# Row sums added on GpSimd and fetched a pair ahead, top-level scores as full products, in a hybrid GLA and NSA layer

## The chip, the core and the metric

The kernel runs on one core of a Trainium2 chip. The metric is device time in microseconds of one execution of the whole layer. Three runs of the kernel before took 1116.94 to 1117.36 us, with a median of 1117.23 us.

The core has TensorE for matrix products, and three engines for elementwise work: VectorE, ScalarE and GpSimd. The profile calls them PE (and PEld for TensorE's weight loads), DVE, ACT and POOL. SyncE (SP) only issues DMA transfers here. Each engine works off its own queue in order, and waits on semaphores for the others.

## The reference

One layer over 256 tokens of width 2048: a gated linear attention (GLA) with 4 heads and a native sparse attention (NSA) with 8 heads read one normalised input through one projection, their outputs go through one output projection, and a SwiGLU feed-forward network (FFN) with 5632 hidden columns follows. Cut to what matters here:

```python
def hybrid_layer(x, ...):
    n = rms_norm(x, attn_norm_g)
    proj = n @ w_in
    ...
    h = x + jnp.concatenate([gla_out, nsa_out], axis=-1) @ w_out
    m = rms_norm(h, ffn_norm_g)
    return h + (jax.nn.silu(m @ w_gate) * (m @ w_up)) @ w_down
```

and of the GLA mixer the scores, which decay with the distance of key and query:

```python
    decay = jnp.exp(jnp.where(causal, b[:, :, :, None, :] - b[:, :, None, :, :], -jnp.inf))
    scores = jnp.einsum('bhtd,bhsd,bhtsd->bhts', qi, ki, decay)
```

## The kernel before

All arrays are fp32. A product of fp32 values is made of three products of a rounded part (hi) and a rest (lo): hi x hi, hi x lo and lo x hi. So each piece of a weight matrix is loaded, rounded by ScalarE (`act(..., AF.Copy)`, lines L136 and L623) and subtracted by VectorE (L137 and L624), before TensorE can use it.

**The stages.** The input projection runs in column blocks of 512 (`proj`), each over four chunks of four row tiles (`chunk`, whose matmuls are L282). The mixers (`gla_mix`, `nsa_mix`) are generators: `drive` (L97) takes a step of them between the matmuls of a chunk, so that their small operations lie under the projections. Then come the output projection (`w_out_half`) and the FFN, which loops over 11 blocks of 512 hidden columns: `gate_up` (products at L1073), `turn_act`, and `down` of the block before (L282 again). In the program's text the operations have this order; the order in each engine's queue is settled when the kernel is built, by a scheduler that may move independent operations past each other. `behind(op)` tells it to place an operation after another.

**Seven products in place of eight.** For a pair of row tiles of the FFN's first product, `gate_up` treats the 2 x 2 tiles of tokens and the 2 x 2 tiles of weights (two of w_gate, two of w_up) as small matrices, and multiplies them with seven products in place of eight (`sevens`). That needs four sums of weight tiles. Where there are none ready, VectorE makes them at the pair (L1104 to L1106): one of 1024 elements a partition and two of 512. `parts_of2` then takes both halves of the sums into hi and lo.

**Row sums made early.** For the blocks 5 to 10 and the pairs 2, 5 and 7 (`SUMS`) these sums are made long before, behind the mixers: 18 generators `sum_rows` (L1003) wait in `background`, and `drive` takes a step of one of them whenever it has counted `rate` units. Each loads two tiles of w_gate and two of w_up from SP's queue (L1009, two transfers of 512 KB), adds in four steps of 512 elements a partition (L1014, on VectorE, each placed behind VectorE's newest subtraction), and stores the two results to DRAM from GpSimd's queue (L1018, two transfers of 512 KB). In the FFN, `gate_up` fetches them back at the pair itself from SP's queue (L1099), right behind the pair's weights (L1041), whose last quarter is then not needed.

**Buffers.** Tiles of 4 KB a partition come from the 24 buffers `g4`. In the FFN, 22 of them are held by the tokens, their forms, the residual and the activations, so that two are left for the first half of a pair's sums; the second half has the two buffers `fsum`. The weights have three buffers `fraw`, their hi and lo parts four buffers `ftwo`.

**GpSimd's other work.** Its queue carries a few masks and memsets, and the power of -1/2 that makes a reciprocal root (`rsqrt_`, L212): 14 short operations on 1 to 8 elements a partition, most of them in the normalisations of the mixers. VectorE waits for each of them.

**Scores by levels.** `gla_scores` (L556) makes the scores of a tile of 128 queries and 128 keys from eight products, one for each level of a binary split (1, 2, 4, to 64), and picks from each the part that belongs to it. Of the top level only the quarter of the 64 first keys and the 64 last queries is used (L574), and only that quarter is computed (L565); the others are full products of 128 x 128 (L567). There are 8 such tiles.

Of the kernel before, what the change touches and what calls it, by code (L numbers as in the profile page):

```python
# [12 lines left out]
ALU = mybir.AluOpType  # L13
AX = mybir.AxisListType

P = 128
# [20 lines left out]
def kernel(  # L37
# [4 lines left out]
    nc = tc.nc  # L42
    act, mm = nc.scalar.activation, nc.tensor.matmul
    TT, TS, STT = nc.vector.tensor_tensor, nc.vector.tensor_scalar, nc.vector.scalar_tensor_tensor
# [13 lines left out]
    def slot(pool, tag, bufs, align=None):  # L58
        def f(shape, dt=F32):
            n_tiles[0] += 1  # L60
            return pool.tile([P] + list(shape), dt, tag=tag, bufs=bufs, name=f"{tag}_{n_tiles[0]}", align_bytes=align)
        return f
# [3 lines left out]
    g4, g2, g1, small = slot(gp, "g4", 24, LINE), slot(s2p, "g2", 13), slot(s1p, "g1", 7), slot(s1p, "sm", 12)  # L66

    def bank():
        n_tiles[0] += 1
        return pp.tile([P, 512], F32, tag="bank", name=f"bank_{n_tiles[0]}")  # L70

    def behind(op):

        return tc.issue_after(op.ins) if op is not None else nullcontext()
# [17 lines left out]
    def drain(queue):  # L92
        while queue:
            for _ in queue.pop(0):
                pass
# [17 lines left out]
    last = {}  # L113
# [442 lines left out]
    def gla_scores(h, b, res):  # L556
        tb = slice(b * P, (b + 1) * P)
        sc, e = g1([P]), dec[h // 2]
        for half in range(2):
            p = bank()  # L560
            for j in range(4):
                l = LEVELS[4 * half + j]
                u, w = (e[l][:, h % 2, tb],) * 2 if l else (kT[:, h, tb], qT[:, h, tb])
                if 2 * l == P:
                    mm(p[:l, j * P + l:(j + 1) * P], u[:, :l], w[:, l:], start=True, stop=True)  # L565
                else:
                    mm(p[:, j * P:(j + 1) * P], u, w, start=True, stop=True)  # L567
                yield
            for j in range(4):
                l, pl = LEVELS[4 * half + j], p[:, j * P:(j + 1) * P]  # L570
                if l == 0:
                    TT(sc, pl, lmask[:, 0, :], ALU.mult)
                elif 2 * l == P:
                    nc.vector.tensor_copy(sc[:l, l:], pl[:l, l:])  # L574
                else:
                    nc.vector.copy_predicated(sc, lmask[:, 4 * half + j, :].bitcast(mybir.dt.uint32), pl)
        res["s"] = sc
# [423 lines left out]
    row_sums = {}  # L1001

    def sum_rows(f, pair):  # L1003

        n_tiles[0] += 1
        gate, up = g4([2, 512]), g4([2, 512])
        for to, m in ((gate, w_gate), (up, w_up)):
            with behind(last["dma"]):
                nc.sync.dma_start(to, m[0][2 * pair * P:(2 * pair + 2) * P, f * FB:(f + 1) * FB].rearrange("(k p) w -> p k w", p=P))  # L1009
        for _ in range(3):  # L1010
            yield True
        for o, i in ((up[:, 0], up[:, 1]), (up[:, 1], gate[:, 1]), (gate[:, 1], up[:, 0]), (gate[:, 0], gate[:, 1])):
            with behind(last["d"]):
                TT(o, o, i, ALU.add)  # L1014
            yield True
        to = row_sums[f, pair] = [dp.tile([P, 2, 512], F32, name=f"sums{i}_{f}_{pair}") for i in range(2)]
        for part, a in zip(to, (up, gate)):
            nc.gpsimd.dma_start(part, a)  # L1018
        for _ in range(1):
            yield True  # L1020
# [3 lines left out]
    fw = {}  # L1024
# [12 lines left out]
    def load4(parts):  # L1037

        r, at = fw["raw"]([4, 512]) if fw else weight("raw", 4, 512, 3, F32), 0
        for mat, k0, nk, c0 in parts:  # L1040
            nc.sync.dma_start(r[:, at:at + nk], mat[k0 * P:(k0 + nk) * P, c0:c0 + 512].rearrange("(k p) w -> p k w", p=P))  # L1041
            at += nk
        return r
# [14 lines left out]
    def parts_of2(s1, s2):  # L1058
# [2 lines left out]
            in_parts(hi[:, 2 * i:2 * i + 2], lo[:, 2 * i:2 * i + 2], v)  # L1061
        return [(hi[:, k], lo[:, k]) for k in range(4)]


    banks = {}

    def gate_up(fb):
        def product(q, a, w, k):

            if q not in banks:  # L1070
                banks[q] = bank()
            for x, m in ((a[0], w[k][0]), (a[0], w[k][1]), (a[1], w[k][0])):
                mm(banks[q], x, m, start=todo[q] == total[q], stop=todo[q] == 1)  # L1073
                todo[q] -= 1

        def tokens(k, t):
            assert k in turned
            return tuple(x[k // 4][:, k % 4, t * P:(t + 1) * P] for x in (hT_h, hT_l))

        order, sevens = (ORDER0, ORDER1, ORDER)[0 if fb == 0 else 1 if fb < ALL7 else 2], FIRST7.get(fb, PAIRS7)  # L1080
        last7 = max(sevens, key=order.index)
        todo = dict.fromkeys((1, 5, 6, 7), 3 * len(sevens))
        todo.update(dict.fromkeys((2, 3, 4), 3 * len(sevens) + 6 * (8 - len(sevens))))
        todo[8] = 6 * (8 - len(sevens))
        total = dict(todo)
        if fb > 1:
            urgent.append(turn_act(fb - 1, (8, 8)))
        for at, pair in enumerate(order):
            if fb > 1 and pair not in sevens:
                drain(urgent)  # L1090
            if fb == 0 and at == len(OLD):
                ffn_pools()
            a, b = 2 * pair, 2 * pair + 1
            ready = row_sums.get((fb, pair))
            r = load4([(w_gate[0], a, 2, fb * FB), (w_up[0], a, 1 if ready else 2, fb * FB)])
            if ready:
                sums = s1, s2 = g4([2, 512]), (fw["sum"] if fw else g4)([2, 512])
                for to, part in zip(sums, ready):
                    nc.sync.dma_start(to, part)  # L1099
            if pair in sevens:  # L1100
                w = parts_of(r[:, 0:3])
                if not ready:
                    s1, s2 = g4([2, 512]), fw["sum"]([2, 512])
                    TT(s1, r[:, 1:3], r[:, 3:4].to_broadcast([P, 2, 512]), ALU.add)  # L1104
                    TT(s2[:, 0], s1[:, 1], r[:, 1], ALU.add)  # L1105
                    TT(s2[:, 1], s2[:, 0], r[:, 0], ALU.add)  # L1106
                f = [tuple(forms[pair][:, i, j] for i in range(2)) for j in range(4)]
                raw = {1: (tokens(b, 0), 1), 2: (tokens(a, 0), 0), 3: (f[3], 2)}
                of_sums = {5: (f[0], 0), 7: (f[2], 1), 6: (f[1], 2), 4: (tokens(a, 1), 3)}

                for q in (6, 1, 5, 7, 2, 3, 4) if at == 7 else (1, 2, 3, 5, 7, 6, 4):
                    if q in of_sums and len(of_sums) == 4:
                        ws = parts_of2(s1, s2)
                        if ready:
                            ws = [ws[k] for k in (1, 0, 3, 2)]
                    if q in raw:
                        x, k = raw[q]
                        product(q, x, w, k)
                    else:
                        x, k = of_sums.pop(q)  # L1120
                        product(q, x, ws, k)
                    yield 2
            else:
                w = parts_of(r)
                for q, t, m in ((2, 0, 0), (3, 0, 1), (4, 1, 0), (8, 1, 1)):
                    for j in range(2):
                        product(q, tokens(a + j, t), w, 2 * m + j)
                        yield 2
            if pair == last7:
                q1, u, q5u, q7u, q57u = (g2([512]) for _ in range(5))  # L1130
                act(q1, banks[1], AF.Copy)
                TT(u, banks[6], q1, ALU.add)
                TT(q5u, banks[5], u, ALU.subtract)
                TT(q7u, banks[7], u, ALU.add)  # L1134
                TT(q57u, banks[5], q7u, ALU.subtract)
                if fb == 1:
                    urgent.append(turn_act(0, (1, 5)))
                if fb:
                    seed(0, DOWN[min(fb - 1, 1)])
        if fb == 0:  # L1140
            drain(urgent)
            rms(rf, ssh)
            TT(rf, rf, hback, ALU.mult)
        gs = hidden[fb] = []
        for t, (g, gq, u_, uq) in enumerate(((q1, 2, q5u, 3), (q7u, 4, q57u, 8))):
            TT(g, banks[gq], g, ALU.add)
            act(g, g, AF.Silu, scale=rf[:, t:t + 1])
            if total[uq]:
                TT(u_, banks[uq], u_, ALU.add)
            STT(g, u_, rf[:, t:t + 1], g, ALU.mult, ALU.mult)  # L1150
            gs.append(g)
# [184 lines left out]
```

## Time and profile before

| | us |
|---|---|
| median of 3 runs | 1117.23 |
| the profiled execution | 1116.86 |
| its span, first to last instruction | 1115.2 |
| TensorE busy (PE) | 1106.1 |
| VectorE busy (DVE) | 993.3 |
| ScalarE busy (ACT) | 741.0 |
| GpSimd busy (POOL) | 50.1 |

The profile is that of one execution. A line of its groups reads: line of the kernel, engine, operation, what it writes and reads by the program's names, shapes, count; then the busy time of the group, the mean duration of one in ns, and the idle time of the engine just before them with what ended it. A line of a timeline gives start, duration, engine, line, operation, and in brackets the idle time before it with its releaser. A line of the chain of waits gives start, duration, and who did the work which the end waited for; followed back from the last instruction, these pieces fill the whole span. "issue" is time in which an engine waited for nothing that the profile shows. A matmul's duration overlaps the next one's, since they are pipelined; two starts lie closer together than the mean duration says. The granted clock of TensorE was 1.00 throughout.

### The profile page before, as it was taken

The page shows a single profiled execution, that of the slowest core. Times are in us where ns is not written, and L with a number is a line of the kernel's source. Part 1 is how long each engine was busy: PE and PEld are TensorE (multiplying, and loading weights), DVE is VectorE, ACT ScalarE, POOL GpSimd, SP SyncE. Part 2 cuts the span into 40 slices and gives each one's busy share as a digit, 9 for nine tenths or more (in the row PEclk, how much of TensorE's full clock was granted, in tenths as well). Part 3 has the DMA queues.
Part 4 walks back from the last instruction along what each step waited for, and adds up shares of the span by engine and source line. Part 5 has one row for each costly group of instructions (what it writes and reads, how often), then busy time and mean ns, then how long its engine had stood idle before and what let it go on. Part 6 is the DMA issues. An engine that isn't in the chain of part 4 may idle for free.

```text
span 1115.2 us, 14712 instructions
## 1 busy us (share of the span) xinstructions
PE 1106.1 (99%) x5354; PEld 908.0 (81%) x5354; DVE 993.3 (89%) x1294; ACT 741.0 (66%) x1001; POOL 50.1 (4%) x97
## 2 busy tenths in 40 slices
PE   9999999999999999999999999999999999999998
PEld 8888887898778887887888888888888788888886
DVE  6678779987588889999899999899999999999997
ACT  7655557544576486657586676768686776768694
POOL 3110000111001000000000000000000000000000
PEclk9999999999999999999999999999999999999999
DMA  7999984475884786646465746767666767766763
GB/s 272 346 343 368 354 284 167 136 247 179 274 303 165 240 303 223 239 175 236 154 214 178 244 159 212 249 227 249 233 245 237 262 207 274 256 245 229 250 226 113
DMA packets 127795, 265.39 MB, mean 238 GB/s; under 512 B 6838, under 2 KB 8922, under 8 KB 127723
## 3 DMA queue, kind: packets, MB, share of 16 engines
q1 hardware_dynamic: 121642, 244.50, 63.4%
q0 software_dynamic: 5184, 18.88, 4.2%
q10 hardware_dynamic: 896, 1.07, 0.3%
q8 instruction: 42, 0.69, 0.2%
q14 instruction: 31, 0.25, 0.1%
HBM read 243.45 MB, written 20.97 MB: 237 GB/s over the span
## 4 chain that ended last, share of the span: by engine, by line
PE 94%; DVE 2%; ACT 2%; DMA 1%; issue 1%; POOL 0%; ACTq 0%; POOLq 0%; DVEq 0%
PE bank L282 46%; PE bank L1073 39%; PE bank L209 3%; PE bank L1214 2%; PE bank L883 1%; PE bank L567 1%; DVE lo L137 1%; PE bank L821 1%; DMA raw<-in_w_in_dram 1%; DMA raw<-in_w_out_dram 0%; ACT hi L136 0%; PE bank L737 0%; ACT ftwo L623 0%; POOL sm L212 0%; PE bank L824 0%
## 5 line engine op out<-in xcount | busy, mean ns | idle before, releaser
L1073 PE MATMUL bank<-ftwo,g 128*128 128x512 f32 x1848 | 431.7, 393 | 0.2 <-ACT ftwo L623 0.2
L1073 PEld LDWEIGHTS bank<-ftwo,g 128*128 128x128 f32 x1848 | 342.0, 188 | 77.1 <-DVE ftwo L624 3.1
L282 PE MATMUL bank<-hi,g 128*128 128x512 f32 (+2 forms) x1088 | 323.5, 376 | 0.0
L624 DVE TENSOR_TENSOR ftwo<-fraw,ftwo 128x1536 fp32r<-128x1536 f32 (+1 forms) x130 | 256.9, 1983 | 7.1 <-ACT ftwo L623 6.1
L623 ACT ACTIVATE ftwo<-fraw 128x1536 fp32r<-128x1536 f32 (+1 forms) x130 | 216.4, 1669 | 26.5 <-DMA fraw<-in_w_up_dram 10.0
L282 PE MATMUL bank<-ftwo,g 128*128 128x512 f32 x960 | 221.2, 390 | 0.4 <-ACT g L623 0.4
L282 PEld LDWEIGHTS bank<-hi,g 128*128 128x128 f32 x1088 | 192.4, 188 | 30.7 <-issue 1.0
L282 PEld LDWEIGHTS bank<-ftwo,g 128*128 128x128 f32 x960 | 179.5, 188 | 39.4 <-ACT bank L1185 1.3
L136 ACT ACTIVATE hi<-raw 128x1024 fp32r<-128x1024 f32 (+3 forms) x124 | 130.1, 1056 | 106.4 <-PE bank L282 62.7
L282 PE MATMUL bank<-lo,g 128*128 128x512 f32 (+3 forms) x544 | 195.3, 377 | 1.2 <-DVE lo L137 1.0
L137 DVE TENSOR_TENSOR lo<-raw,hi 128x1024 fp32r<-128x1024 f32 (+3 forms) x124 | 150.1, 1218 | 37.1 <-ACT hi L136 32.3
L623 ACT ACTIVATE ftwo<-g 128x1024 fp32r<-128x1024 f32 x74 | 78.3, 1058 | 75.9 <-DVE g L1104 60.4
L282 PEld LDWEIGHTS bank<-lo,g 128*128 128x128 f32 x544 | 98.5, 188 | 16.9 <-DVE lo L137 2.0
L624 DVE TENSOR_TENSOR ftwo<-g,ftwo 128x1024 fp32r<-128x1024 f32 x74 | 90.3, 1220 | 15.7 <-ACT ftwo L623 15.7
L624 DVE TENSOR_TENSOR ftwo<-fsum,ftwo 128x1024 fp32r<-128x1024 f32 x74 | 90.3, 1220 | 0.3
L623 ACT ACTIVATE ftwo<-fsum 128x1024 fp32r<-128x1024 f32 x74 | 77.6, 1050 | 4.5 <-DVE fsum L1106 3.3
L1197 ACT COPY g<-bank 128x512 f32<-128x512 f32 x80 | 46.0, 587 | 43.8 <-PE bank L282 41.9
L1104 DVE TENSOR_TENSOR g<-fraw 128x1024 f32<-128x1024 f32 x54 | 65.3, 1219 | 0.3 <-issue 0.3
L1185 ACT COPY bank<-g 128x512 f32<-128x512 f32 x80 | 45.0, 590 | 10.7 <-DVE f L1134 9.1
L623 ACT ACTIVATE g<-bank 128x512 fp32r<-128x512 f32 (+1 forms) x50 | 29.0, 591 | 32.8 <-PE bank L209 22.3
L1106 DVE TENSOR_TENSOR fsum<-fsum,fraw 128x512 f32<-128x512 f32 x54 | 37.2, 688 | 0.8
L1105 DVE TENSOR_TENSOR fsum<-g,fraw 128x512 f32<-128x512 f32 x54 | 37.1, 688 | 0.8
(235 smaller groups left out, 873.8 us busy)
## 6 DMA issues: line engine op xcount, KB each, us to landing
fraw<-in_w_gate_dram SPq DMA_DIRECT2D x86, 512.0 KB, 3.7
fraw<-in_w_down_dram SPq DMA_DIRECT2D x42, 1024.0 KB, 5.1
raw<-in_w_in_dram SPq DMA_DIRECT2D x36, 1024.0 KB, 6.9
fraw<-in_w_up_dram SPq DMA_DIRECT2D x68, 512.0 KB, 4.7
sums<-g POOLq DMA_DIRECT2D x36, 512.0 KB, 6.6
raw<-in_w_out_dram SPq DMA_DIRECT2D x16, 1024.0 KB, 6.2
g<-in_w_gate_dram SPq DMA_DIRECT2D x18, 512.0 KB, 7.6
g<-in_w_up_dram SPq DMA_DIRECT2D x18, 512.0 KB, 8.2
```

What stands on the lines that cost most here:

```text
L136: act(h[:, i:i + n], r[:, k + i:k + i + n], AF.Copy)
L137: last["d"] = TT(o[:, i:i + n], r[:, k + i:k + i + n], f32(h[:, i:i + n]), ALU.subtract)
L209: return nc.tensor.transpose(o, i, ident[:n, :n])
L282: last["mm"] = mm(bk[t], a[:, k, t * P:(t + 1) * P], m[:, off:off + w], start=(first_ and k == 0 and i == 0), stop=(end and k == 3 and i = ...
L623: act(hi, ps, AF.Copy)
L624: last["d"] = TT(lo, ps, f32(hi), ALU.subtract)
L1073: mm(banks[q], x, m, start=todo[q] == total[q], stop=todo[q] == 1)
L1104: TT(s1, r[:, 1:3], r[:, 3:4].to_broadcast([P, 2, 512]), ALU.add)
L1105: TT(s2[:, 0], s1[:, 1], r[:, 1], ALU.add)
L1106: TT(s2[:, 1], s2[:, 0], r[:, 0], ALU.add)
L1185: nc.scalar.copy(banks[qs[n][t]], h_sb[n][:, t, :])
L1197: nc.scalar.copy(h_sb[n][:, t, :], bs[t])
```

## The change

Three edits:

- The four additions of `sum_rows` run on GpSimd in place of VectorE, and are no longer placed behind an operation of VectorE.
- The sums are fetched by `fetch_sums`, from GpSimd's queue in place of SP's, and a pair ahead: at the start of a pair, for the pair after it. The buffers for them are taken then.
- The top level's score product is computed in full (128 x 128) like the others; the part that is used stays the same.

```diff
@@ gla_scores
-                if 2 * l == P:
-                    mm(p[:l, j * P + l:(j + 1) * P], u[:, :l], w[:, l:], start=True, stop=True)
-                else:
-                    mm(p[:, j * P:(j + 1) * P], u, w, start=True, stop=True)
+                mm(p[:, j * P:(j + 1) * P], u, w, start=True, stop=True)
@@ sum_rows
         for o, i in ((up[:, 0], up[:, 1]), (up[:, 1], gate[:, 1]), (gate[:, 1], up[:, 0]), (gate[:, 0], gate[:, 1])):
-            with behind(last["d"]):
-                TT(o, o, i, ALU.add)
+            nc.gpsimd.tensor_tensor(o, o, i, ALU.add)
             yield True
@@ new
+    fetched = {}
+
+    def fetch_sums(fb, pair):
+
+        if (fb, pair) in row_sums:
+            to = fetched[fb, pair] = g4([2, 512]), fw["sum"]([2, 512])
+            for a, part in zip(to, row_sums[fb, pair]):
+                nc.gpsimd.dma_start(a, part)
@@ gate_up
             ready = row_sums.get((fb, pair))
+            if at < 7:
+                fetch_sums(fb, order[at + 1])
             r = load4([(w_gate[0], a, 2, fb * FB), (w_up[0], a, 1 if ready else 2, fb * FB)])
             if ready:
-                sums = s1, s2 = g4([2, 512]), (fw["sum"] if fw else g4)([2, 512])
-                for to, part in zip(sums, ready):
-                    nc.sync.dma_start(to, part)
+                s1, s2 = fetched.pop((fb, pair))
```

The new lines shift the numbers of the lines behind them: L1014 becomes L1010, L1018 becomes L1014, L624 becomes L621.

## The prediction

> **What bounds the kernel now.** I read the page's first part and its chain of waits, then the busy time by stretch, then the chain in order of time.
>
> ```profile
> span 1115.2 us, 14712 instructions
> PE 1106.1 (99%) x5354; PEld 908.0 (81%) x5354; DVE 993.3 (89%) x1294; ACT 741.0 (66%) x1001; POOL 50.1 (4%) x97
> PE 94%; DVE 2%; ACT 2%; DMA 1%; issue 1%; POOL 0%; ACTq 0%; POOLq 0%; DVEq 0%
> ```
> ```profile
> 40.00:160.00 120.00, 120.00 (x549) 99.12 (x548) 92.10 (x126) 67.73 (x83) 9.76 (x18) 1.00 0.94 343
> 160.00:240.00 80.00, 79.04 (x496) 69.08 (x495) 70.40 (x177) 46.20 (x94) 8.19 (x9) 1.00 0.59 193
> 240.00:345.00 105.00, 104.29 (x634) 82.94 (x633) 79.33 (x193) 59.80 (x153) 11.73 (x15) 1.00 0.65 221
> 515.00:1067.00 552.00, 551.99 (x2453) 450.39 (x2453) 528.43 (x479) 397.80 (x425) 0.00 (x0) 1.00 0.65 228
> ```
> ```profile
> 945.19 21.80 PE bank L282 x96
> ...
> 1006.39 21.79 PE bank L282 x96
> ```
>
> TensorE ends the run: 94% of the chain is its own work. In the stretches the columns after the length are busy time of PE, weight load, DVE, ACT and POOL. From 515 to 1067 us (the FFN) PE is idle for 0.01 us in 552, and one block of 512 hidden columns repeats every 61.2 us (945.19 to 1006.39). So nothing that helps VectorE can be earned there; it can only be lost, since VectorE has 528.43 of 552. Of the mixers, 160 to 240 us is the stretch to watch: VectorE 70.40 of 80, and the chain leaves TensorE.
>
> ```profile
> 188.16 0.26 PE bank L565 x2
> ...
> 190.67 0.22 PE bank L567 x2
> ...
> 210.96 1.17 DVE lo L137
> ...
> 212.49 0.69 POOL sm L212
> 213.19 2.39 issue
> ...
> 215.62 1.41 POOL sm L212
> ...
> 217.28 1.19 DVE lo L137
> ```
>
> Between 210.96 and 218.47 the end waits for VectorE's queue (the lo parts of L137), and VectorE for two of GpSimd's rsqrt (L212).
>
> **The edits, and what the trace has of them.**
>
> ```profile
> L1014 DVE TENSOR_TENSOR g<-g,g 128x512 f32<-128x512 f32 x36 | 24.7, 686 | 0.4
> L1014 DVE TENSOR_TENSOR g<-g 128x512 f32<-128x512 f32 x36 | 24.5, 686 | 8.0 <-DMA g<-in_w_up_dram 7.8
> ```
> ```profile
> L1014 DVE TENSOR_TENSOR g<-g,g 128x512 f32<-128x512 f32 x4 | 2.7, 686 | 0.0
> L1014 DVE TENSOR_TENSOR g<-g 128x512 f32<-128x512 f32 x3 | 2.0, 682 | 0.0
> ```
> ```profile
> L1014 DVE TENSOR_TENSOR g<-g 128x512 f32<-128x512 f32 x3 | 2.1, 685 | 0.0
> ...
> L1014 DVE TENSOR_TENSOR g<-g,g 128x512 f32<-128x512 f32 x2 | 1.4, 681 | 0.0
> ```
> ```profile
> L867 POOL MEMSET g<- 128x512 f32 x8 | 4.0, 545 | 0.0
> L398 POOL TENSOR_SCALAR_AFFINE_SELECT g<-g 128x256 f32<-128x256 f32 x1 | 0.5, 490 | 0.1
> ```
> ```profile
> 193.97 1.62 POOL L212 TENSOR_TENSOR sm<-sm,mhalf 128x2 f32<-128x2 f32 x1 [16.93 <-DVE sm L600]
> ...
> 215.62 1.40 POOL L212 TENSOR_TENSOR sm<-sm,mhalf 128x2 f32<-128x2 f32 x1 [2.43 <-DVE sm L693]
> ...
> 221.79 2.13 POOL L212 TENSOR_TENSOR sm<-sm,mhalf 128x2 f32<-128x2 f32 x1
> ...
> 239.88 0.71 POOL L212 TENSOR_TENSOR sm<-sm,mhalf 128x2 f32<-128x2 f32 x1 [12.13 <-DVE sm L600]
> ```
> ```profile
> 215.45 0.68 DVE L1014 TENSOR_TENSOR g<-g 128x512 f32<-128x512 f32 x1
> 216.05 0.41 DVE L607 TENSOR_TENSOR g<-g,g 128x256 f32<-128x256 f32 x1
> ...
> 222.08 1.27 DVE L137 TENSOR_TENSOR lo<-raw,hi 128x1072 fp32r<-128x1072 f32 x1
> ```
>
> (1) Removed from VectorE: 72 adds x 0.686 = 49.4 us, all before the FFN. Where VectorE runs ahead this is worth nothing: from 40 to 160 us PE is busy 120.00 of 120. It can pay only between about 160 and 345 us.
>
> (2) Added to GpSimd: 72 adds of 128x512. The trace has no such add. From below: GpSimd's affine select, one operand in and one out, took 490 ns for 256 elements, so 0.98 us for 512. From above: another operand costs at most another such pass, taken as the memset's 0.545 us, so 1.5 us. I take 1.15 us, nearer the select; 72 make 83 us beside GpSimd's 50.1 us of work, in 390 us of mixers: GpSimd itself is no bound.
>
> (3) The two engines get in each other's way. The same rsqrt of two elements takes 0.71 us at 239.88, and 1.40 and 2.13 us at 215.62 and 221.79, where VectorE runs operations with both inputs in SBUF: at 215.62 it ends 0.56 us after L607, at 221.79 0.57 us after L137. So GpSimd waited for VectorE. That VectorE waits in turn for a long add of GpSimd isn't in the trace; per add the cost to VectorE lies between 0 (gaps, or operations on PSUM) and 1.15 us. SBUF — State Buffer of the Trainium skill, section "Who interferes with whom", says that a VectorE instruction with two SBUF inputs contends with a GpSimd instruction that reads SBUF, and that whoever issues first holds the pair until it ends: the rsqrt rows agree for GpSimd's side, and by it each add could cost VectorE up to its whole length. I take 0.95 us where VectorE is packed, near the upper end, because its queue there is mostly subtractions and multiplications from SBUF. The packed stretches hold 12 of the 72 adds (second and third fence of this part: 4 + 3 from 160 to 240 us, 3 + 2 from 300 to 345 us): 12 x (0.95 - 0.686) = +3.2 us, bounds 12 x (0 - 0.686) = -8.2 and 12 x (1.15 - 0.686) = +5.6. A gain is held by what the chain gives to others there: 210.96 to 218.47 is 7.5 us, of which two L137 (2.4) and two unstretched rsqrt (1.4) stay; so I cut the lower bound to -3.7 us. GPSIMD Engine Reference of the Trainium skill, section "Elementwise — side-by-side cycle accounting", measures an add of 2048 fp32 elements at 4497 ns on GpSimd; a quarter, 1.12 us, is an estimate, and by it the sum would be the same.
>
> (4) GpSimd's queue is in order, and the adds have lost their place behind VectorE's work. Better: with L1014 gone from 215.45, the rsqrt at 215.62 isn't stretched: -0.7 us. Worse: a rsqrt now stands behind a whole group.
>
> ```profile
> 226.40 0.68 SPq L1009 DMA_DIRECT2D g<-in_w_up_dram  x1
> ```
> ```profile
> L1018 POOL DMA_DIRECT2D sums<-g x36: 531/531/720, 42.7 to 432.2; - x36
> ...
> DMA to landing us min/median/max: 2.9/6.6/9.6
> ```
> ```profile
> DMA to landing us min/median/max: 5.8/8.2/11.3
> ```
>
> (The last row is that of the loads of L1009.) The group loaded at 226.40 lands between 232.2 and 237.7; in the built order its four adds and two stores stand ahead of the rsqrt that was asked for at 239.88. At the late end GpSimd is free at 237.7 + 4 x 1.15 + 2 x 0.53 = 243.4, 3.5 us late, and VectorE's queue stands with L137 behind it. Bounds 0 and +3.5; I take +0.5, since VectorE has a quarter of 240 to 345 us free (79.33 of 105) to catch up. SP's later loads of L1009 now also wait for GpSimd to be done with a buffer; the order of these loads is unchanged, and I cost it at nothing, covered by the three raw tiles of L125.
>
> (5) Fetches: 36 transfers of 512 KB leave SP and go to GpSimd, a pair earlier.
>
> ```profile
> 869.34 0.33 SPq L1099 DMA_DIRECT2D g<-sums  x1
> ```
> ```profile
> 878.65 1.22 DVE L624 TENSOR_TENSOR ftwo<-g,ftwo 128x1024 fp32r<-128x1024 f32 x1
> ```
> ```profile
> 878.79 2.15 PEld L1073 LDWEIGHTS bank<-ftwo,g 128*128 128x128 f32 x10 [0.23 <-DVE ftwo L624]
> ```
> ```profile
> PEld bank L1073 <- DVE ftwo L624: 2.1, 11, 0.3
> ```
> ```profile
> L623 ACT ACTIVATE ftwo<-g 128x1024 fp32r<-128x1024 f32 x74 | 78.3, 1058 | 75.9 <-DVE g L1104 60.4
> ```
>
> GpSimd executes nothing else in the FFN. For pair 7 the buffers set the issue: the fetch at 869.34 went out when VectorE had read pair 5's sums, and that doesn't change, because there are still two such buffers. It is wanted by ScalarE's copy (L623, 1058 ns) some 1.1 us before 878.65, so there are 8.2 us; GpSimd's transfers took 6.6 in the median and 9.6 at worst. Pairs 2 and 5 go out earlier than before. I cost it at 0. Without that cover PE waits at once, as the 0.23 us shows: up to 1.4 us in each of six blocks, +8.4 us. The other bound is -2.1, if all the weight loads' waits for L624 from 700 to 1067 us (11, 2.1 us) vanish.
>
> (6) Top-level scores: eight products, full instead of a quarter. In the chain two passes of the quarter (L565) hold PE 0.26 us and two of a full one (L567) 0.22. So 8 x -0.04 = -0.3; were the full ones 0.04 dearer, +0.3. I take 0.
>
> **Sum.** +3.2 - 0.7 + 0.5 + 0 + 0 = +3.0 us. The profiled execution took 1116.86 us (span 1115.2); the median of the runs, 1117.23, is 0.37 above it. Forecast for the median: 1117.23 + 3.0 = 1120.2 us. About 0.2% (2.2 us) is what a measurement of this kernel can tell from no change, so this is slower, which begins at 1119.5.
>
> **The rivals.**
> - Relief wins. The adds fall into VectorE's gaps, VectorE is ahead at 195 to 220 us, and the end gets back what the chain lost there. For it: from 240 to 345 us VectorE has 25.7 us free. Against: 70.40 of 80 from 160 to 240. It decides if an add costs VectorE under about 0.4 us. Worth the -3.7 us of (3): 1113.5.
> - It cancels, or the mixers' reserve swallows both: 1117.2. For it: PE idles only 0.96 us from 160 to 240 us.
> - GpSimd starves: at 221.79 the rsqrt sat out operations of VectorE that followed each other without a gap. Four adds that starve so hold the queue; two rsqrt (asked for at 193.97 and 239.88) then come a group late, 4 x 1.15 + 2 x 0.53 = 5.7 us each, with L137 behind them: +11.4, 1128.6. It decides once a group takes about twice its 4.6 us.
> - The fetches for pair 7 come late: six blocks by 1.0 us, under the worst of 1.4: +6.0, 1123.2. For it: the 9.6 us at worst; against: the issue of GpSimd's transfers is hardly ever stretched (531 ns in the median, 720 at most). SBUF — State Buffer of the Trainium skill, section "SBUF: two separate sides", says that GpSimd can't write descriptors while VectorE runs in a two-port mode; those issue rows show nothing of it.
>
> **Chances.** Forecast 0.42 (its own range 1119 to 1124), relief 0.20, cancels 0.16, starves 0.14, late fetches 0.08. Slower by over 0.2%: 0.42 less 0.02 for its lower edge, plus 0.14 and 0.08 = 0.62; same 0.16 + 0.02 = 0.18; faster 0.20. Range 1113.0 to 1127.0: it takes in the relief, with 0.5 us to spare, and late fetches, and leaves out the far half of starving.
>
> **What would show it.** VectorE's busy time falls by less than 49 us, because its operations beside GpSimd's adds get longer (L137 over 1.27 us); adds of about 1.15 us, longer beside VectorE; the block in the FFN still 61.2 us; the loss between 160 and 345 us. I'm wrong if VectorE's other operations keep their lengths, or if the FFN block changes by over 0.3 us.

## The result, and the profile after

| | before | after |
|---|---|---|
| median of 4 runs, us | 1117.09 | 1131.96 |
| lowest to highest, us | 1116.74 to 1117.36 | 1131.53 to 1134.90 |
| the profiled execution, us | 1116.86 | 1131.58 |

The changed kernel is slower: the ratio of the times is 1.0136, with a 95% interval of 1.0125 to 1.0148. That is 14.9 us, where 3.0 were forecast, and above the forecast's range.

The page of the changed kernel: span, busy time of the engines, and the groups of the subtraction L137 and of the adds (L1010, which were L1014).

```profile
span 1129.9 us, 14732 instructions
PE 1108.6 (98%) x5354; PEld 909.6 (81%) x5354; DVE 990.6 (88%) x1222; ACT 744.2 (66%) x1001; POOL 182.1 (16%) x205
L137 DVE TENSOR_TENSOR lo<-raw,hi 128x1024 fp32r<-128x1024 f32 (+3 forms) x124 | 173.8, 1410 | 61.7 <-ACT hi L136 61.3
L1010 POOL TENSOR_TENSOR g<-g 128x512 f32<-128x512 f32 x36 | 56.2, 1565 | 139.6 <-DMA g<-in_w_up_dram 116.5
L1010 POOL TENSOR_TENSOR g<-g,g 128x512 f32<-128x512 f32 x36 | 58.4, 1621 | 2.6
```

The same L137 in the kernel before:

```profile
L137 DVE TENSOR_TENSOR lo<-raw,hi 128x1024 fp32r<-128x1024 f32 (+3 forms) x124 | 150.1, 1218 | 37.1 <-ACT hi L136 32.3
```

VectorE lost 72 instructions of 49.4 us together, and its busy time fell by 2.7 us (993.3 to 990.6). Its other work grew by the difference of 46.7 us, or 0.65 us for each add on GpSimd. Half of that (23.7 us, 150.1 to 173.8) is the subtraction L137.

Busy time by stretch (PE, weight load, VectorE, ScalarE, GpSimd, then the granted clock), first after, then two stretches of before that the prediction didn't show:

```profile
40.00:160.00 120.00, 118.67 (x542) 97.92 (x541) 85.46 (x86) 67.23 (x82) 70.97 (x57) 1.00 0.95 334
160.00:240.00 80.00, 76.97 (x486) 68.43 (x484) 73.93 (x168) 46.58 (x90) 22.84 (x20) 1.00 0.62 209
240.00:345.00 105.00, 101.58 (x613) 80.89 (x612) 75.61 (x174) 55.51 (x139) 26.54 (x25) 0.98 0.67 228
345.00:435.00 90.00, 85.74 (x411) 67.99 (x410) 73.38 (x131) 56.34 (x109) 29.60 (x26) 0.98 0.68 239
435.00:515.00 80.00, 76.61 (x337) 61.88 (x336) 73.37 (x82) 48.32 (x50) 1.95 (x3) 1.00 0.52 173
515.00:1067.00 552.00, 551.61 (x2453) 449.59 (x2452) 527.30 (x481) 399.15 (x427) 18.89 (x36) 1.00 0.68 229
```
```profile
345.00:435.00 90.00, 88.88 (x428) 70.99 (x427) 78.99 (x153) 59.87 (x109) 8.77 (x16) 1.00 0.74 262
435.00:515.00 80.00, 79.35 (x351) 64.41 (x350) 77.46 (x80) 50.09 (x43) 0.00 (x0) 1.00 0.61 211
```

In the FFN TensorE is busy nearly as before (551.61 of 552, 551.99 before). TensorE loses time in every stretch ahead of it, and most from 240 to 515 us; there the granted clock also falls to 0.98 in two stretches.

Matmuls of L282 come in nearly the same order in both kernels. The start of the n-th one against the n-th one of before shows where the run falls back (worked out from the starts in the two traces):

| n-th matmul of L282, and its start before | 600: 131.7 us | 624: 138.1 | 720: 160.9 | 840: 201.5 | 1320: 322.6 | 1368: 342.2 | 1584: 412.4 | 1608: 418.6 | 1700: 527.6 |
|---|---|---|---|---|---|---|---|---|---|
| later in the changed kernel by, us | 0.1 | 1.6 | 3.6 | 3.7 | 2.2 | 6.4 | 6.7 | 12.2 | 14.9 |

The loss comes in jumps, at about 133, 161, 188, 338, 422 and 437 us. The largest one in VectorE's timeline of the changed kernel (start, duration):

```profile
412.11 2.07 DVE L137 TENSOR_TENSOR lo<-raw,hi 128x1024 fp32r<-128x1024 f32 x1 [1.85 <-ACT hi L136]
414.11 1.39 DVE L949 TENSOR_TENSOR g<-g 128x128 f32<-128x128 f32 x1
415.42 0.28 DVE L951 TENSOR_TENSOR g<-g 128x128 f32<-128x128 f32 x1
415.62 1.78 DVE L621 TENSOR_TENSOR g<-g,g 128x512 fp32r<-128x512 f32 x1
417.32 1.54 DVE L950 TENSOR_TENSOR g<-g,g 128x128 f32<-128x128 f32 x1
...
420.24 0.69 DVE L621 TENSOR_TENSOR g<-g,g 128x512 fp32r<-128x512 f32 x1
420.84 0.28 DVE L949 TENSOR_TENSOR g<-g 128x128 f32<-128x128 f32 x1
...
423.99 1.28 DVE L917 TENSOR_TENSOR g<-bank,g 128x512 f32<-128x512 f32 x2
```

In the same time GpSimd does the adds of group 16 (the 18 generators of `sum_rows` are counted from 0 in the order of `background`, four adds each):

```profile
413.18 3.67 POOL L1010 TENSOR_TENSOR g<-g,g 128x512 f32<-128x512 f32 x2
...
417.40 1.30 POOL L1010 TENSOR_TENSOR g<-g 128x512 f32<-128x512 f32 x1
```

And TensorE:

```profile
422.29 0.39 PE L282 MATMUL bank<-hi,g 128*128 128x512 f32 x1
426.09 0.33 PE L209 MATMUL bank<-ident,g 128*128 128x128 f32 x1 [3.42 <-ACT g L977]
```

L949 to L952 (`pair_forms`) work on 128 elements a partition. Where no add runs, they take 0.28 us (L949 at 420.84). Beside the adds, L949 takes 1.39 and L950 1.54 us: each was held for about the length of one add (1.30 us at 417.40), and so were L621 (1.78, of 0.69 at 420.24) and L137 (2.07, of 1.22). L951 at 415.42 was not held: here it was the add that took longer (the two of 413.18 take 3.67 us together). Together these four cost 1.11 + 1.26 + 1.09 + 0.85 = 4.3 us within one group. VectorE works in order, so the residual addition L917 is that much late (the run with memsets below shows the same row of operations without the waits); ScalarE's scaling (L977) and the transposes (L209) wait for it, and TensorE stands for 3.42 us.

Rows of the view by windows for this place, in windows of one microsecond (the granted clock is the third number from the end; behind it stand the busy share of the DMA engines and GB/s):

```profile
425.00:426.00 1.00, 0.00 (x0) 0.00 (x0) 1.00 (x2) 1.00 (x4) 0.00 (x0) 1.00 1.06 412
426.00:427.00 1.00, 0.91 (x3) 0.39 (x3) 0.40 (x1) 1.00 (x4) 0.00 (x0) 0.69 1.05 406
427.00:428.00 1.00, 0.90 (x3) 0.52 (x3) 0.00 (x0) 1.00 (x2) 0.00 (x0) 0.50 1.05 408
428.00:429.00 1.00, 1.00 (x5) 0.88 (x4) 0.75 (x1) 0.53 (x2) 0.75 (x1) 0.50 1.06 410
429.00:430.00 1.00, 1.00 (x6) 0.70 (x5) 0.91 (x2) 0.97 (x3) 1.00 (x1) 0.60 1.04 403
```

Behind the stall the granted clock is 0.50 for 3.4 us, which costs TensorE another 1.7 us (0.31 + 0.50 + 0.50 + 0.40). The same follows the stall at 338 us, where TensorE is idle from 338.97 to 341.62; the clock is halved from 341.05 to 344.46, 0.57 us of it in the stall, so there it costs 1.4 us. The chain of waits for that place:

```profile
336.40 4.57 DVE g L848 x6
340.97 0.61 DVE g L621
```

Six of VectorE's tensor_scalar L848 (0.34 us each where GpSimd does nothing) take 4.57 us there, in the time of group 13. By the timelines of the two engines only one of the six is held by an add (1.37 us, at 337.85). Three others stand beside GpSimd's other work: 1.60 us (at 336.32) beside the issue of a store and two memsets (L864), 0.71 us beside the issue of the other store, 0.69 us beside one more memset. So of the 3 us that these six lose, about 2 go to other work of GpSimd than the adds.

By these rows about 3.1 us of the 14.9 (1.7 + 1.4, an estimate) are a lower clock.

### The profile page after: what moved, and what is told of

It reads as the page before. It is cut to its first block, busy times and chain, and to the rows that moved or that the text cites. A ratio compares the mean times of both kernels' runs of the same rounds, so it can differ in the third digit from the quotient of the medians.

```text
span 1129.9 us, 14732 instructions
## 1 busy us (share of the span) xinstructions
PE 1108.6 (98%) x5354; PEld 909.6 (81%) x5354; DVE 990.6 (88%) x1222; ACT 744.2 (66%) x1001; POOL 182.1 (16%) x205
## 4 chain that ended last, share of the span: by engine, by line
PE 67%; DVE 1%; DMA 1%; POOL 1%; ACT 1%; issue 0%; POOLq 0%; DVEq 0%
PE bank L1078 38%; PE bank L282 24%; PE bank L1219 2%; PE bank L209 2%; PE bank L880 1%; POOL g L1010 1%; DMA g<-in_w_up_dram 1%; DVE g L848 0%; PE bank L818 0%; ACT ftwo L620 0%; DMA sums<-g 0%; DVE lo L137 0%; ACT g L977 0%; DVE g L621 0%; ACT f L1152 0%
## 5 line engine op out<-in xcount | busy, mean ns | idle before, releaser
L282 PE MATMUL bank<-hi,g 128*128 128x512 f32 (+2 forms) x1088 | 327.4, 378 | 0.0
L621 DVE TENSOR_TENSOR ftwo<-fraw,ftwo 128x1536 fp32r<-128x1536 f32 (+1 forms) x130 | 257.2, 1984 | 7.6 <-ACT ftwo L620 7.2
L137 DVE TENSOR_TENSOR lo<-raw,hi 128x1024 fp32r<-128x1024 f32 (+3 forms) x124 | 173.8, 1410 | 61.7 <-ACT hi L136 61.3
L282 PE MATMUL bank<-ftwo,g 128*128 128x512 f32 x960 | 221.2, 390 | 0.4 <-ACT g L620 0.4
L282 PEld LDWEIGHTS bank<-hi,g 128*128 128x128 f32 x1088 | 193.2, 189 | 30.2 <-issue 1.0
L282 PEld LDWEIGHTS bank<-ftwo,g 128*128 128x128 f32 x960 | 179.7, 188 | 39.0 <-ACT bank L1190 0.9
L282 PE MATMUL bank<-lo,g 128*128 128x512 f32 (+3 forms) x544 | 196.0, 379 | 2.8 <-DVE lo L137 2.5
L282 PEld LDWEIGHTS bank<-lo,g 128*128 128x128 f32 x544 | 98.9, 189 | 18.3 <-DVE lo L137 3.4
L621 DVE TENSOR_TENSOR ftwo<-g,ftwo 128x1024 fp32r<-128x1024 f32 x74 | 90.3, 1220 | 13.7 <-ACT ftwo L620 13.7
L1067 POOL DMA_DIRECT2D g<-sums x18 | 9.6, 533 | 554.4 <-DVE ftwo L621 525.8
L621 DVE TENSOR_TENSOR ftwo<-fsum,ftwo 128x1024 fp32r<-128x1024 f32 x74 | 90.2, 1220 | 2.8 <-ACT ftwo L620 2.7
L1010 POOL TENSOR_TENSOR g<-g 128x512 f32<-128x512 f32 x36 | 56.2, 1565 | 139.6 <-DMA g<-in_w_up_dram 116.5
L1010 POOL TENSOR_TENSOR g<-g,g 128x512 f32<-128x512 f32 x36 | 58.4, 1621 | 2.6
L1190 ACT COPY bank<-g 128x512 f32<-128x512 f32 x80 | 45.1, 591 | 11.4 <-DVE f L1139 9.4
```

What stands on the lines that cost most here:

```text
L137: last["d"] = TT(o[:, i:i + n], r[:, k + i:k + i + n], f32(h[:, i:i + n]), ALU.subtract)
L282: last["mm"] = mm(bk[t], a[:, k, t * P:(t + 1) * P], m[:, off:off + w], start=(first_ and k == 0 and i == 0), stop=(end and k == 3 and i = ...
L621: last["d"] = TT(lo, ps, f32(hi), ALU.subtract)
L1010: nc.gpsimd.tensor_tensor(o, o, i, ALU.add)
L1190: nc.scalar.copy(banks[qs[n][t]], h_sb[n][:, t, :])
```

## The experiments

Three theories were open. C: the adds hold up VectorE's operations that read SBUF (the on-chip memory in which the engines' tiles lie; a `bank` lies in another one, PSUM). Q: GpSimd's longer groups hold its queue and the buffers. F: the moved fetch or the full score products carry a part. Ratios are against the kernel before, run on the same chip.

| run | what runs where | median, us | ratio, 95% interval |
|---|---|---|---|
| adds_back | all but the adds moved | 1115.34 | 0.9983 (0.9973 to 0.9992) |
| adds_alone | only the adds moved | 1136.00 | 1.0172 (1.0157 to 1.0187) |
| scores_alone | only the full products | 1115.85 | 0.9984 (0.9974 to 0.9994) |
| fetch_alone | only the fetch moved | 1117.50 | 0.9999 (0.9990 to 1.0009) |
| no_adds | the change, no adds anywhere | 1116.96 | 0.9992 (0.9982 to 1.0002) |
| memsets | the change, memsets for adds | 1112.65 | 0.9958 (0.9943 to 0.9973) |
| copies | the change, copies for adds | 1127.17 | 1.0079 (1.0052 to 1.0107) |
| halves | the change, adds cut in two | 1136.88 | 1.0177 (1.0154 to 1.0200) |
| late_on_vector | groups 0 to 9 on GpSimd | 1118.12 | 1.0007 (0.9996 to 1.0018) |
| early_on_vector | groups 10 to 17 on GpSimd | 1134.63 | 1.0144 (1.0127 to 1.0162) |
| last_two_on_vector | groups 0 to 15 on GpSimd | 1126.43 | 1.0072 (1.0055 to 1.0089) |
| paced | adds_back, groups at other times | 1123.35 | 1.0058 (1.0036 to 1.0081) |

### The three edits apart

adds_back is the changed kernel with

```diff
-            nc.gpsimd.tensor_tensor(o, o, i, ALU.add)
+            with behind(last["d"]):
+                TT(o, o, i, ALU.add)
```

> The changed kernel with the 72 adds back on VectorE; the fetch a pair ahead from GpSimd's queue and the full score products stay. Theory C (the adds on GpSimd hold up VectorE's operations that read SBUF, and that is the whole loss): 1116 to 1118.5 us, the VectorE subtraction of 128x1024 back from 1410 to about 1220 ns in the mean of its line, no stretch with a granted clock under 1.00. Rival F (the moved fetch or the full products carry a part of the loss): 1120 us or more.

adds_alone is the kernel before with the opposite edit.

> The kernel before with only the 72 adds moved to GpSimd. Theory C: 1130 to 1134 us, like the changed kernel, with the two stalls of TensorE near 338 and 422 us and half the clock behind each. Rival F: under 1128 us.

scores_alone and fetch_alone are the kernel before with one of the other two edits as the change has it.

> The kernel before with only the full top-level score products. Theory S (a product on a quarter of the array lets TensorE stand about 0.25 us before and behind it, eight times, and this stretch has no reserve): 1114.8 to 1115.6 us, 2 us under the kernel before. Rival F2 (the 2 us that the changed kernel with its adds back on VectorE gained come from the fetch): within 0.7 us of the kernel before.

> The kernel before with only the fetch of the sums a pair ahead from GpSimd's queue. Theory S, and the prediction's step (5) with a cost of 0: 1116.6 to 1118 us. Rival F2: 1115.5 us or less.

The adds carry the whole loss: with them back on VectorE the time is 1115.34 us, L137 takes 1219 ns in the mean, and the clock is 1.00 throughout. This version is faster than both kernels, against the one before by 0.17%, and lies under the 1116 us that were expected at least. The adds alone cost a little more than expected, 1136.00 us. The fetch is worth nothing that can be measured, and the full products save 1.6 us alone (1115.85, where 1115.6 was the upper end of what was expected). In the start of the n-th matmul of L282, adds_back leaves the kernel before between the matmuls 744 (before's 167.4 us; 0.1 us later) and 1128 (262.7 us; 2.2 us earlier), which is where the scores are computed. One of the eight places in TensorE's timeline, first before, then scores_alone:

```profile
183.44 0.40 PE L282 MATMUL bank<-hi,g 128*128 128x512 f32 x1
183.77 0.33 PE L565 MATMUL bank<-g 128*64 128x64 f32 x2
184.03 0.50 PE L282 MATMUL bank<-hi,g 128*128 128x512 f32 x1
```
```profile
183.32 0.39 PE L282 MATMUL bank<-hi,g 128*128 128x512 f32 x1
183.55 0.38 PE L564 MATMUL bank<-g 128*128 128x128 f32 x2
183.69 0.48 PE L282 MATMUL bank<-hi,g 128*128 128x512 f32 x1
```

From the matmul ahead to the matmul behind the quarter takes 0.59 us, the full product 0.37. The two passes themselves start 0.11 us apart in both; the quarter starts 0.10 us later behind the matmul ahead, and the next matmul 0.12 us later behind it. Six of the eight places differ by 0.20 to 0.22 us, the other two by 0.13 and 0.01; together that is 1.4 us of the 1.6 (worked out from the starts in the two traces). TensorEngine Tiling (Array Packing) of the Trainium skill, section "Key Properties", says that changing the tiling mode drains TensorE; the starts agree, with 0.10 us ahead of the quarter (128*64) and 0.12 us behind it, between full ones.

### Is it the reading of SBUF or the queue?

no_adds leaves the adds out, and memsets puts three writes of about the same length together in their place:

```diff
-            nc.gpsimd.tensor_tensor(o, o, i, ALU.add)
+            for _ in range(3):
+                nc.gpsimd.memset(o, 0.0)
```

> The changed kernel without the 72 adds on any engine: the loads, stores and fetches stay, the sums are left out. It is the change with VectorE's relief and without any cost on GpSimd. Theory C: VectorE's operations keep the lengths of before (subtraction 1220 ns), and the time is 1112 to 1117 us, which is what the relief is worth alone. Rival Q (what costs is GpSimd's queue and the late buffers, set by the loads and stores): 1120 us or more.

> The changed kernel with each add replaced by three GpSimd memsets of the same 128x512 result (3 x 545 = 1635 ns, where an add took 1565 to 1621 ns in the mean): the sums are left out, GpSimd's queue and the buffers are held as long, but nothing reads SBUF there. Theory C: VectorE's subtraction stays at about 1220 ns and the time is 1112 to 1119 us. Rival Q: the same 1220 ns, and still 1126 us or more. If memsets hold up VectorE as adds do, the subtraction is over 1300 ns and the time over 1125 us; then this run says nothing on Q.

GpSimd's work in the run with memsets, and the ends of the row of VectorE's operations that the changed kernel has from 412.11 to 423.99 us, here beside the memsets of the same group:

```profile
L1011 POOL MEMSET g<- 128x512 f32 x216 | 102.5, 527 | 154.8 <-DMA g<-in_w_gate_dram 142.8 <-PE bank L282 8.2 <-DMA g<-in_w_up_dram 3.7
```
```profile
402.05 1.22 DVE L137 TENSOR_TENSOR lo<-raw,hi 128x1024 fp32r<-128x1024 f32 x1 [1.85 <-ACT hi L136]
...
409.61 1.28 DVE L917 TENSOR_TENSOR g<-bank,g 128x512 f32<-128x512 f32 x2
```

From this L137 to L917 the same operations in the same order take 7.56 us here and 11.88 in the changed kernel: the 4.3 us that the adds of one group cost VectorE. The memsets hold GpSimd for 102.5 us (the adds 56.2 + 58.4 = 114.6), with the same loads, stores and buffers, and the time is 1112.65 us: no loss, and L137 at 1219 ns. So Q falls, and with it the idea that GpSimd's rsqrt come late. What is held beside memsets here are a few operations with one tensor, by 4 us in all: tensor_scalar L848 (1.53 us beside three memsets) and a copy L545 (1.41 us) among them. By this run C's price is 1131.96 - 1112.65 = 19.3 us, and the relief of VectorE is worth 1115.34 - 1112.65 = 2.7 us.

One place of the changed kernel speaks for Q at first sight: its chain of waits goes from 421.87 to 438.84 us through group 17 itself, its load (6.22 us), its adds and a store (2.88 us) that gives a buffer back to L621. But VectorE was busy up to that point (L952 from 438.69 to 438.97), so there the two end together; and in the run with memsets, which keeps that load and that store, nothing is lost.

no_adds came out slower than memsets, at the upper end of what was expected; measured against it, C's price would be 15.0 us, and there would be no relief. Nearly all of the difference arises between the matmuls 1128 and 1320 of L282 (no_adds is 2.9 us ahead of the kernel before at the first and 0.5 us behind it at the second, memsets 3.1 and 3.6 us ahead). In its chain of waits a load of w_out ends what TensorE waits for there.

```profile
301.49 12.37 DMA raw<-in_w_out_dram
```

Without anything in the adds' place, the stores of the sums go out at once; that they slow this load wasn't tried. So 19.3 and 2.7 us are the terms with the loads and stores held back nearly as in the changed kernel.

copies has two GpSimd copies in place of each add, so one operand is read where an add reads two:

```diff
-            nc.gpsimd.tensor_tensor(o, o, i, ALU.add)
+            for _ in range(2):
+                nc.gpsimd.tensor_copy(o, i)
```

> The changed kernel with each GpSimd add replaced by two GpSimd copies of the same 128x512 operand to the same result: the sums are left out, and each GpSimd instruction reads one operand of SBUF instead of two. If reading SBUF is enough to hold up VectorE: its subtraction of 128x1024 over 1300 ns in the mean and 1124 us or more. If only an instruction with two operands does it: 1220 ns and 1112 to 1116 us, as with memsets.

```profile
L1011 POOL COPY g<-g 128x512 f32<-128x512 f32 x144 | 120.2, 841 | 144.2 <-DMA g<-in_w_up_dram 118.1
```

L137 is 1333 ns in the mean, and the time 1127.17 us (1122.84 to 1129.78 in the four runs): reading one operand from SBUF is enough. SBUF — State Buffer of the Trainium skill, section "Who interferes with whom", says just this (a GpSimd instruction that reads SBUF contends with a VectorE instruction that has two inputs there, one that only writes does not), and the three runs agree: adds 1131.96, copies 1127.17, memsets 1112.65 us.

### How long is an operation held?

halves cuts each add:

```diff
-            nc.gpsimd.tensor_tensor(o, o, i, ALU.add)
+            for c in range(0, 512, 256):
+                nc.gpsimd.tensor_tensor(o[:, c:c + 256], o[:, c:c + 256], i[:, c:c + 256], ALU.add)
```

> The changed kernel with each GpSimd add cut in two of 256 elements (144 adds of about 0.7 us). Theory L (a VectorE operation that meets an add waits until that instruction ends): the short operations L949 to L952, up to 1.82 us beside an add in the changed kernel and 0.28 alone, stay under 1.1 us; each late group costs VectorE less, and the time is 1120 to 1129 us. Rival B (the two engines share the port at a rate, however the work is cut): L949 to L952 as long as in the changed kernel or longer, 1130 us or more.

VectorE's timeline in that run, beside group 16:

```profile
414.75 0.82 DVE L949 TENSOR_TENSOR g<-g 128x128 f32<-128x128 f32 x1
415.50 0.83 DVE L951 TENSOR_TENSOR g<-g 128x128 f32<-128x128 f32 x1
416.25 1.23 DVE L621 TENSOR_TENSOR g<-g,g 128x512 fp32r<-128x512 f32 x1
417.39 0.82 DVE L950 TENSOR_TENSOR g<-g,g 128x128 f32<-128x128 f32 x1
```

Theory L was right on the operations and wrong on the time. Each is held by 0.54 us (0.28 to 0.82) in place of 0.9 to 1.5, so a VectorE operation waits until the instruction it has met ends, as that theory has it. But now these four and the four behind them are all held, and the two engines take turns: 4.2 us in the group, as much as with whole adds. Over the run 62 of VectorE's operations are held in place of 51, by 38 us in all in place of 42 (worked out from the traces: those over 0.1 us longer than the same operation is in adds_back and no_adds). The time is 1136.88 us. Shorter instructions on GpSimd make each wait shorter, and the waits more. Why the run is 4.9 us longer with a little less waiting isn't shown; 4.0 us of it are there by the 720th matmul of L282 (7.6 us behind the kernel before, where the changed kernel is 3.6).

### Which groups cost

In late_on_vector, early_on_vector and last_two_on_vector the adds go to GpSimd only for some of the 18 groups (the condition is `< 10`, `>= 10` and `< 16`):

```diff
-            nc.gpsimd.tensor_tensor(o, o, i, ALU.add)
+            if 3 * (f - ALL7) + SUMS.index(pair) < 10:
+                nc.gpsimd.tensor_tensor(o, o, i, ALU.add)
+            else:
+                with behind(last["d"]):
+                    TT(o, o, i, ALU.add)
```

> The changed kernel with the adds of the groups 0 to 9 (to 164 us) on GpSimd and those of the groups 10 to 17 on VectorE again. Theory C (the late groups hold up a packed VectorE): the loss at 338 and 422 to 442 us is gone, the one at 133 and 161 us stays (1.5 and 1.0 us less what comes back): 1115.5 to 1118.5 us, granted clock 1.00 in every stretch. Rival: a late group costs by its loads and buffers, whoever adds: 1125 us or more.

> The changed kernel with the adds of the groups 0 to 9 on VectorE again and those of the groups 10 to 17 on GpSimd. Theory C: 1128 to 1132 us, with stalls of TensorE near 338 and 422 us and half the clock behind them. Rival (the loss comes from all groups alike): about 10/18 of it is gone, 1122 to 1125 us.

> The changed kernel with the adds of the last two groups alone (16 and 17, from 412 us on) on VectorE again. In the changed kernel TensorE fell back by 6.7 us up to 412 us and by 14.8 us up to 453 us. Theory C: those 8 us come from these eight adds beside the short operations L949 to L952 and from the half clock behind the stall, and go: 1122.5 to 1126 us, with no stall over 1.5 us after 412 us, and the stall at 338 us still there. Rival (VectorE then stands at the head of its queue for the loads of these groups, as it did in the paced kernel): 1128 us or more.

early_on_vector came out above its range (1134.63, where 1132 was the upper end). Against adds_back (1115.34), the ten early groups cost 2.8 us and the eight late ones 19.3, though VectorE's operations are held by the same 22 us in both (counted as above: 23 of them in the one, 26 in the other). The two don't add up to the 16.6 us of all 18: beside the late groups the early ones cost nothing that can be measured (the runs, 1131.10 to 1135.23 and 1131.53 to 1134.90, overlap). The early ones meet L137, which is 18.1 us of the 22 (168.2 us, 150.1 before). Their one large stall in late_on_vector, on VectorE and on TensorE:

```profile
131.91 2.77 DVE L137 TENSOR_TENSOR lo<-raw,hi 128x1024 fp32r<-128x1024 f32 x1 [1.13 <-ACT hi L136]
```
```profile
136.88 0.33 PE L209 MATMUL bank<-ident,g 128*128 128x128 f32 x1 [2.87 <-ACT g L505]
```

Half the clock followed it here, where 1.00 was expected. Not in each run: five of the ten had a mean clock of 1.000 and took 1116.73 to 1117.39 us, the other five 0.998 and 1118.85 to 1120.65. In early_on_vector L137 takes 1232 ns in the mean, almost as before, and the loss is there all the same:

```profile
425.60 0.47 PE L209 MATMUL bank<-ident,g 128*128 128x128 f32 x1 [3.96 <-ACT g L977]
```

So L137's 23.7 us, half of what VectorE's work grew by, cost little, and what costs is short operations that stand in a row ahead of something urgent.

The windows from 300 us on tell the last two groups apart; first the changed kernel, then last_two_on_vector, then adds_back:

```profile
300.00:405.00 105.00, 100.85 (x561) 79.50 (x560) 81.82 (x181) 61.90 (x133) 35.48 (x32) 0.98 0.67 240
405.00:455.00 50.00, 43.09 (x190) 33.07 (x188) 41.22 (x56) 33.12 (x55) 15.80 (x13) 0.97 0.58 211
```
```profile
300.00:405.00 105.00, 100.86 (x552) 79.05 (x552) 81.10 (x178) 60.05 (x141) 34.84 (x32) 0.97 0.66 236
405.00:455.00 50.00, 48.70 (x226) 38.57 (x225) 44.59 (x74) 40.09 (x65) 2.88 (x5) 1.00 0.68 244
```
```profile
405.00:455.00 50.00, 48.79 (x220) 39.01 (x219) 47.57 (x66) 36.40 (x51) 2.84 (x5) 1.00 0.71 252
```

With the eight adds of these groups back on VectorE, TensorE gets back 5.6 us of busy time between 405 and 455 us (43.09 to 48.70), and the clock; from 300 to 405 us its busy time stays. Counted by the matmuls of L282, the changed kernel loses 8.2 us behind the 1584th (6.7 to 14.9), this one 0.1 (12.0 to 12.1). The median fell by only 5.5 us, a little less than the 6 to 9.5 expected; the profiled execution is the slowest of the four (1129.32 us) and had lost 12.0 us by that matmul.

### A try at a better version

```diff
-    rate[0] = 30
-    drive([proj(C_KC, ev_kc), proj(C_KS, ev_kv(0)),
-           proj(C_KW, ev_kv(1), ((0, 256), (256, 280))), proj(C_NQ, ev_nq(0))], 2.5)
+    rate[0] = 0
+    drive([proj(C_KC, ev_kc), proj(C_KS, ev_kv(0))], 2.5)
+    rate[0] = 14
+    drive([proj(C_KW, ev_kv(1), ((0, 256), (256, 280))), proj(C_NQ, ev_nq(0))], 2.5)
```

> The changed kernel with its adds back on VectorE, and the early sums paced otherwise: no steps during the first two projections of the second stage (about 160 to 222 us, where VectorE is packed), and steps every 14 units during the next two (222 to 285 us) in place of every 30 in all four. If VectorE's packed stretch between 160 and 222 us is what the adds there cost: 1113.5 to 1115 us, about 1 us under the kernel with the adds back on VectorE and no other pacing. If the adds there cost nothing: the same as that kernel, 1115.3.

It went the other way, 1123.35 us. VectorE's timeline:

```profile
252.87 1.22 DVE L137 TENSOR_TENSOR lo<-raw,hi 128x1024 fp32r<-128x1024 f32 x1
256.93 0.69 DVE L1011 TENSOR_TENSOR g<-g 128x512 f32<-128x512 f32 x1 [2.85 <-DMA g<-in_w_up_dram]
```

An add on VectorE waits for its load at the head of the queue, here for 2.85 us, with the score operations behind it; TensorE then stood for 4.08 us. On GpSimd such a wait holds only GpSimd. No version that makes the sums is faster than adds_back, and scores_alone is as fast (0.9984 and 0.9983 of the kernel before).

## Why the prediction was wrong, step by step

The direction and the mechanism were right: slower, because GpSimd's adds and VectorE's operations from SBUF hold each other. The size was off by five times, because the step that priced this counted the wrong adds and left out what a burst of them does.

- **(1)** Relief from 40 to 160 us is worth nothing: right (PE busy 120.00 of 120 in adds_back and in the run with memsets alike). That nothing can be lost there either, which the sum took for granted, was wrong by 2.8 us (late_on_vector).
- **(2)** An add takes 1.28 to 1.30 us where it isn't held, against 1.15 forecast; with its own waits 1.57 and 1.62 in the mean, over the upper bound of 1.5. That GpSimd itself is no bound was right.
- **(3)** This is the step that failed: "12 x (0.95 - 0.686) = +3.2 us". The relief in it, 12 x 0.686 = 8.2 us, was worth 2.7. The conflict in it, 12 x 0.95 = 11.4 us, was 19.3. Even its upper bound of +5.6 was a third of the net 16.6. Two things made it too small. It counted 12 adds, in the stretches where VectorE was packed and TensorE already waited, 160 to 240 and 300 to 345 us, and left out everything behind 345 us. There VectorE had 78.99 of 90 us and TensorE 88.88: no idle time to show, but no reserve either, and over half of the loss arose there (6.4 to 14.9 us later). The 32 adds of the groups 10 to 17 alone cost 19.3 us (early_on_vector against adds_back). And it priced an add alone. Four come in a row, VectorE's queue is held for 4.3 us in one group, and the stall of 3.42 us brought half the clock for 3.4 us on top, which no row of the trace of before shows.
- **(4)** The rsqrt and the buffers: nothing, as the run with memsets shows. The rival in which GpSimd starves named 1128.6 us, but its mechanism (two rsqrt a group late) isn't what happened: it was VectorE that had to wait.
- **(5)** The fetch at 0: right (0.9999).
- **(6)** The full products at 0, bounds -0.3 to +0.3: wrong. They save 1.6 us alone. The chain's rows gave 0.26 against 0.22 us for two passes, and the step took these rows for the whole price; the starts of the matmuls around them in the trace of before (183.44, 183.77, 184.03) show what the quarter costs ahead of it and behind it.

The terms as measured close within 0.6 us: 1117.4 (before, beside these runs) - 1.6 (products) + 0.1 (fetch) - 2.7 (relief) + 19.3 (conflict) = 1132.5, beside 1131.96. That tests the products and the fetch alone (1115.9, beside adds_back's 1115.34): relief and conflict are both differences to the run with memsets.

Of the signs, VectorE's came out (busy time 2.7 us less in place of 49, L137 1.41 us), and so did the FFN. The loss didn't lie between 160 and 345 us: 3.6 us were lost ahead of it and 8.5 behind it.

The rival "relief wins" would have been the result if GpSimd's instruction read no SBUF: memsets ran 1112.65 us, beside its 1113.5. The nearness is in part luck: 1.6 us of it are the products, and the relief was 2.7 us where it had 3.7.

## What to carry to other kernels

Before work moves to GpSimd, look for short VectorE operations with two SBUF inputs, and for tensor_scalar and copies, that run in the same time and stand ahead of something urgent: each can be held for the whole length of the GpSimd instruction, whatever its own length (L949, 0.28 us alone, took 1.39). Cutting the GpSimd work finer didn't help here. A stretch in which TensorE is busy throughout isn't a reserve; ask how far VectorE is ahead there, and whether that covers a whole burst. And a product of an odd shape between full ones should be priced with the gaps around it, not by its own rows.

## What was not expected of the hardware

- The clock falls after much shorter stalls than expected, and not after each. TensorE: Matmul & The Clock Gate of the Trainium skill, section "What's actually happening", gives one idle window of about 3.4 us, free-running. In these runs an idle time of 1.29 us (no_adds, at 315 us), 1.94 (copies, at 340) and 2.66 (after, at 338) was followed by half the clock, and 1.75 (after, at 188), 2.54 (adds_alone, at 134) and 2.77 (early_on_vector, at 190) was not. The starts of the matmuls, their ends (which are modelled) and the granted clock in all the traces, from 40 to 1000 us, tell more. The falls of one trace lie whole multiples of 3.413 us apart (in the changed kernel 341.05 and 426.38 us, 25 of them), so the windows of 3.41 us between them can be laid out. In the window right ahead of each of the 18 falls TensorE was idle for 1.83 to 3.13 us in all, several stalls taken together (1.96 in no_adds); of the windows at full clock without a fall behind them only one had over 1.80 us (1.94, adds_alone at 133 us). The 2.77 us fell into two windows, 1.28 and 1.80 us. So what counts here is the idle time within one window, from about 1.8 us on: the 3.41 us agree with that page of the Trainium skill, a whole idle window isn't needed. Once the clock fell, it was 0.50 for 3.4 us in 15 of the 18 cases and for 6.8 us in three, so one fall costs about 1.7 us or more where TensorE has work throughout.
- VectorE's tensor_scalar L848 with one tensor and a scalar a partition, 0.34 us alone at 128x256, took 1.39 and 1.37 us beside adds, 1.60 us beside the issue of a transfer and two memsets, and 0.69 us beside one memset. So it isn't only operations with two tensors from SBUF that are held, and this one is held by memsets too (SBUF — State Buffer of the Trainium skill, section "Who interferes with whom", names tensor_scalar among those that can take both ports). The operations from PSUM in the same time kept their lengths (L489, a scalar_tensor_tensor of 128x255: 478 ns in the mean before, 474 after; copy_predicated of 128x128: 297 and 298).
